# Longer pauses in the chain that makes the second FFN block's factors

## The chip, the core and the metric

The kernel runs on one core of a Trainium2 chip. Its engines each work through their own row of instructions, in the order in which the program gives them: TensorE (PE, matmuls, and PEld for its weight loads), VectorE (DVE), ScalarE (ACT), GpSimd (POOL) and SyncE (SP), which here issues all DMA transfers. The metric is device time in microseconds (us); less is better.

## The reference

One layer of a streaming encoder over 2048 prompt frames and 64 sample frames, 2112 tokens of width 1024: a gated delta-rule group and a pooling group with a common output projection, then a SwiGLU feed-forward part (FFN) of inner width 2816. The change touches the FFN and what prepares it.

```python
x = x + jnp.concatenate([o_delta, o_pool], axis=-1) @ w_out
h = rmsnorm(x, norm2_w)
x = x + (jax.nn.silu(h @ w_gate) * (h @ w_up)) @ w_down
```

All is computed in float32. Each operand of a matmul is split into a high part (a cast to float32r) and the rest, and three matmuls make one product.

## The kernel before

**Blocks and features.** The FFN runs over three blocks of 704 tokens, each in two halves of 352. The inner width is cut into 22 features of 128 columns. For a feature, gate and up are made together as a 2 x 2 by 2 x 2 product in Strassen's way (Winograd's form): seven products of 12 matmuls of 128x352 instead of eight, with three accumulators `px`, `py` and `pz` (`gate_up`, L1606). A product may be added to `px` again only after the sum so far has been copied out: ACT copies it to `g` or `u` (`COPY g<-px`), DVE adds the rest later, ACT makes the sigmoid in three steps (`ACTIVATE hr`), and DVE multiplies into `hr`.

**Weights.** A feature's weights come by DMA as raw tiles (`wr`, loads `wr<-in_wg_dram` and `wr<-in_wu_dram`). In the first block POOL makes the four sums S1 to S4 of them (`wrS`), ACT casts each to its high part, DVE subtracts for the low part (`ws`, `wsS`), and SP stores the split sums to DRAM (`gS<-wsS`) for the later blocks. Raw and split tiles live in small sets of buffers: a load or a cast waits until the old content has been read, and where the old content is also stored, until that store has landed (`prep_strassen`, L614).

**Down projection.** After every two features POOL makes four sums of the finished `hr` (`q<-hr`, and one in place), which ACT and DVE split into factors `hq` (`factors`, L1666). Groups of four features (one of two) are then multiplied by the down weights. For most groups this too is done in Strassen's way, with split sums that were made beforehand and are loaded straight from DRAM (`wsdS<-dsd`), beside raw tiles `wrd` that ACT and DVE split to `wsd` (`load_down`, L675). Group zero is features 0 to 3, group one 4 to 7, group two 8 to 11, group three 12 to 15. In the first block groups one to three are multiplied one feature pair late: group one follows feature 9, group two feature 13.

**The chain.** A block needs its tokens normalised and combined before its first feature: four row pairs of tiles, each with the seven factors 11, T1, T2, 21, T3, 22, T4. For the second block this runs as a chain of steps beside the first block's features (`stats2`, L1416, called by `between`, L1715, from feature 2 on). After the sums of squares, each of four turns (k = 0 to 3) loads four tiles (`xd<-x2d`), scales them on DVE (`xd<-xd,nw,r`), makes four differences on POOL (`xt<-xd,xd`, `xd<-xd,xd`, `xt<-xd,xt`) and stores seven tiles (`hpd<-xd`, `hpd<-xt`). The tiles come from a set of four buffers (`XBUFS["xs"]`). The second block reads them back through `load_h` (L1504) after the last feature of the first.

**What sets the order.** The program is not emitted as written. Every operation is noted by a recording layer (`Machine`), which places the operations of all engines with costs of its own, each engine taking the operation of lowest rank among those it holds ready; rank is mostly the place in the written order. Where the chain's steps are written is set by pauses: a chain gives back a number of us (`yield LAT_APPLY`, L1437 to L1457, five in each turn), and its next step is written once that much of matmul time has been written on PE. `LAT_APPLY` is 1.69.

Of the kernel before, what the change touches and what calls it, by code (L numbers as in the profile page):

```python
# [11 lines left out]
F32 = mybir.dt.float32  # L12
F32R = mybir.dt.float32r
# [5 lines left out]
P = 128  # L19
D = 1024  # L20
KT = D // P
# [19 lines left out]
TB2 = NTOK // NB2  # L41
# [3 lines left out]
PX = PB[0] + 2 * HP + DEC  # L45
# [322 lines left out]
def hybrid_kernel(ctx, tc, a, o):  # L368
# [128 lines left out]
    for G in FGROUPS:  # L497
        groups.append((f0, G))
        f0 += G
    plan, pres = [], [("pre", m, *groups[gi]) for gi in PRE[0] for m in range(KT // 2)]  # L500

    def with_pres(j, keys):

# [7 lines left out]
    for j in range(NBLK):  # L511
# [5 lines left out]
        else:  # L517
# [8 lines left out]

    dsd = {(f0, m): dpool.tile([4, P, 512], F32, tag=f"dsd{f0}_{m}", name=f"dsd{f0}_{m}")
           for f0, G in (groups[gi] for gi in PRE[0]) for m in range(KT // 2 * G // 4)}

    def halves(b, gi):  # L530

# [32 lines left out]
    def prep():  # L564
        key = plan[state["at"]]
        state["at"] += 1
        if key[0] == "pre":
            return pre_down(*key[1:])
        if key in stored and key[0] != "gu":
            parts = []  # L570
            for i in range(2):
                t = wtiles(f"p{i}")[1]()
                nc.sync.dma_start(out=flat(t), in_=wsd[key[0]][key[1], i])
                parts.append(t)
        elif key[0] == "wl":
            raw, parts = (f() for f in wtiles("l"))
            nc.sync.dma_start(out=raw, in_=wpd[key[1]] if key[2] else a["wout"][key[1]][:, :512])
            wsplit(parts, raw)
        elif key[0] in ("win", "wout"):
            parts = []  # L580
            for i in range(2):
                raw, t = (f() for f in wtiles(f"p{i}"))
                src = a[key[0]][key[1]][:, 512 * i : 512 * i + 512]
                nc.sync.dma_start(out=raw, in_=wpd[key[1]] if key[0] == "wout" and i else src)
                if key == ("win", 0):

                    r3, h3, l3 = (x.rearrange("p (k c) -> p k c", c=P) for x in (raw, t[:, 0], t[:, 1]))
                    nc.gpsimd.memset(l3[:, :, 64:].bitcast(F32), 0.0)
                    nc.scalar.copy(l3[:, :, :64], r3[:, :, :64])
                    nc.scalar.copy(h3[:, :, :64], r3[:, :, :64])  # L590
                    tt(h3[:, :, 64:], r3[:, :, 64:], l3[:, :, :64].bitcast(F32), ALU.subtract)
                else:
                    wsplit(t, raw)
                parts.append(t)
            if len(key) == 2:
                due.append((key, [(wsd[key[0]][key[1], i], t) for i, t in enumerate(parts)]))
        elif key[0] == "dn":
            _, m, f0, G = key
            raw, parts = (f() for f in wtiles("d", m % 2 == 0))
            nc.sync.dma_start(out=raw[:, : G * P], in_=a["wd"][m][:, f0 * P : (f0 + G) * P])  # L600
            wsplit(parts, raw, G * P, nc.vector)
        elif key[0] == "ds":
            parts = load_down(*key[1:4]) if key[4] else prep_down(*key[1:4])
        else:
            parts = prep_strassen(key)
        ready.append((key, parts))

        while due and due[0][0] != key:
            k, done = due.pop(0)
            for dst, t in done:  # L610
                nc.sync.dma_start(out=dst, in_=flat(t))
            stored.add(k)

    def prep_strassen(key):  # L614

        q = {f"{i}{j}": a[nm][key[1]][:, (j - 1) * 512 : j * 512]
             for i, nm in ((1, "wg"), (2, "wu")) for j in (1, 2)}
        raw, t, old = {}, {}, key in stored

        def get(nm, src):  # L620
            raw[nm] = wtiles(nm)[0]()
            nc.sync.dma_start(out=raw[nm], in_=q[src])

        if old:
            for i, nm in enumerate(FW):
                t[nm] = wtiles(nm, i % 2 == 1)[1]()
                if nm in gsd:
# [12 lines left out]
        gt(out=raw["S2"], in0=raw["S1"], in1=raw["11"], op=ALU.subtract)  # L640
        gt(out=raw["S4"], in0=raw["12"], in1=raw["S2"], op=ALU.subtract)
        for i, nm in enumerate(FW):
            t[nm] = wtiles(nm, i % 2 == 1)[1]()
            wsplit(t[nm], raw[nm], 512, nc.vector)
        due.append((key, [(gsd[nm][key[1]], t[nm]) for nm in FW if nm in gsd]))
        return t

    def pre_down(m, f0, G):

        n, was = G // 2 * P, machine.boost  # L650
        machine.boost = -PRE_LATE
        (tl, tr), (ll, lr) = ([t[:, i * n : i * n + n] for i in range(2)] for t in (
            names["poolw"], gp.tile([P, PX], F32, tag="pw", name=f"pr{f0}_{m}", bufs=2)[:, :512]))
        for t, m0 in ((tl, m), (ll, m + KT // 2)):
            both = bass.AP(t.tensor, t.offset, [list(t.ap[0]), [1, 2 * n]])
            nc.sync.dma_start(out=both, in_=a["wd"][m0][:, f0 * P : (f0 + G) * P])
# [7 lines left out]
        for i, x in enumerate((ll, lr, tl, tr)):  # L664
            parts = spare[i % len(spare)]
            split_w(parts.rearrange("p (q n) -> p q n", q=2), x)
            nc.sync.dma_start(out=dsd[f0, m][i], in_=parts.bitcast(F32))
        machine.boost = was

    def split_w(t, x):  # L670

# [744 lines left out]
    def stats2(b, pool, tag, tbufs):  # L1416

        r = cpool.tile([P, TB2], F32, tag="r", name=f"r{b}")
        src = stream_x(x2d, f"xd{b}_", TB2 * b)
        yield from rstd(f"n2_{b}", r, src, SUBS2, pool, tag, tbufs, nc.gpsimd)  # L1420
        yield 4.0
        gt = nc.gpsimd.tensor_tensor

        def put(nm, k, t):
            nc.sync.dma_start(out=hpd[b, FH.index(nm), k], in_=t)

        def get(k, i):
            t = src(k, N2 * i, N2)
            stt(t, t, n2w[:, k : k + 1], r[:, N2 * i : N2 * i + N2], ALU.mult, ALU.mult)
            return t  # L1430

        def new(nm, k):
            return wpool.tile([P, 512], F32, tag="xs", name=f"x{nm}{k}_{b}", bufs=XBUFS["xs"])[:, :N2]

        for k in range(4):
            b12, b22 = get(k, 1), get(k + 4, 1)
            yield LAT_APPLY  # L1437
            t3 = new("t3", k)
            gt(out=t3, in0=b22, in1=b12, op=ALU.subtract)
# [7 lines left out]
            yield LAT_APPLY  # L1447
# [5 lines left out]
            yield LAT_APPLY  # L1453
            t4 = new("t4", k)
            gt(out=t4, in0=b21, in1=t2, op=ALU.subtract)
            put("T4", k, t4)
            yield LAT_APPLY  # L1457

    heads = []
    blocks = []  # L1460
# [247 lines left out]


    fpos = {2: (0, 1), 4: (0, 2, 1, 3)}  # L1710
    six = [opool.tile([P, 3, 2, TB2], F32R, tag="op", name=f"h3_{i}", bufs=2) for i in range(2)]
    h3t = [six[i // 3][:, i % 3] for i in range(6)]
    h3, ys = {}, {}

    def between(b):  # L1715
# [78 lines left out]

STORE = 300e3

SLACK = 0.6
# [118 lines left out]
```

## Time and profile before

| | us |
|---|---|
| median of three runs | 2304.91 (2303.8 to 2306.77) |
| the profiled execution, as timed | 2305.54 |
| its span in the profile | 2303.8 |
| mean granted TensorE clock | 0.997 of full speed |

The profile is one execution. In its rows, buffer numbers are left out (`wsS<-wrS,wsS` is any split of a sum). A row in order of time gives start, length, engine, operation, tiles, how many in a row, and in brackets how long the engine had been idle before and what released it. A stretch gives each engine's busy time and, in brackets, its number of instructions. Between two stretches PE can be busy to the same share and have done fewer matmuls, because a matmul's record grows with a slow clock; the counts show it.

### The profile page before, as it was taken

The page shows a single profiled execution, that of the slowest core. Times are in us where ns is not written, and L with a number is a line of the kernel's source. Part 1 is how long each engine was busy: PE and PEld are TensorE (multiplying, and loading weights), DVE is VectorE, ACT ScalarE, POOL GpSimd, SP SyncE. Part 2 cuts the span into 40 slices and gives each one's busy share as a digit, 9 for nine tenths or more (in the row PEclk, how much of TensorE's full clock was granted, in tenths as well). Part 3 has the DMA queues.
Part 4 walks back from the last instruction along what each step waited for, and adds up shares of the span by engine and source line. Part 5 has one row for each costly group of instructions (what it writes and reads, how often), then busy time and mean ns, then how long its engine had stood idle before and what let it go on. Part 6 is the DMA issues. An engine that isn't in the chain of part 4 may idle for free.

```text
span 2303.8 us, 41539 instructions
## 1 busy us (share of the span) xinstructions
PE 2274.5 (99%) x14518; PEld 2134.6 (93%) x14518; DVE 1709.6 (74%) x3131; ACT 1342.5 (58%) x3036; POOL 829.9 (36%) x891
## 2 busy tenths in 40 slices
PE   8999999999999999999999999999999999999998
PEld 7998898888787888999999999999999999999998
DVE  7989866685678796788788777866667768666676
ACT  6987866684769864555346456554344574353344
POOL 3425342453246450555344236622111353010112
PEclk9999999999999999999999999999999999999999
DMA  8765586578476777867776578789765776666663
GB/s 287 262 187 188 203 292 233 194 238 275 158 248 230 213 211 256 304 239 247 256 258 223 187 254 294 254 262 313 241 192 199 261 279 225 210 216 224 210 196 104
DMA packets 256515, 536.96 MB, mean 233 GB/s; under 512 B 30001, under 2 KB 94001, under 8 KB 256305
## 3 DMA queue, kind: packets, MB, share of 16 engines
q1 hardware_dynamic: 256304, 534.30, 68.9%
q8 instruction: 114, 1.87, 0.3%
q14 instruction: 97, 0.79, 0.1%
HBM read 403.62 MB, written 130.58 MB: 232 GB/s over the span
## 4 chain that ended last, share of the span: by engine, by line
PE 91%; DVE 5%; ACT 1%; DMA 1%; issue 1%; POOL 1%; SPq 0%; POOLq 0%; DVEq 0%; ACTq 0%
PE px L283 21%; PE pp L283 18%; PE pz L283 13%; PE py L283 10%; PE dx L283 9%; PE dy L283 4%; PE d L283 3%; PE dz L283 2%; PE pk_p L283 2%; PE pt_p L283 2%; PE gr_p L283 1%; DVE y L283 1%; PE py_p L283 1%; DVE h L283 0%; PE px_p L283 0%
## 5 line engine op out<-in xcount | busy, mean ns | idle before, releaser
L283 PE MATMUL pp<-h,wsp 128*128 128x512 f32 (+1 forms) x2480 | 548.2, 364 | 10.5 <-DVE wsp L283 10.5
L283 PEld LDWEIGHTS pp<-h,wsp 128*128 128x128 f32 x2480 | 401.7, 190 | 58.9 <-ACT wsp L283 10.2
L283 ACT CAST ws<-wr 128x512 fp32r<-128x512 f32 x198 | 122.3, 618 | 172.1 <-PE dx L283 56.7
L283 DVE TENSOR_TENSOR ws<-wr,ws 128x512 fp32r<-128x512 f32 x198 | 170.3, 863 | 36.0 <-ACT ws L283 30.9
L283 POOL TENSOR_TENSOR q<-hr,hr 128x352 f32<-128x352 f32 x52 | 59.1, 1136 | 373.7 <-DVE hr L283 365.5
L283 ACT CAST wsd<-wrd 128x512 fp32r<-128x512 f32 (+1 forms) x120 | 62.5, 526 | 185.6 <-PE dx L283 65.9
L283 PE MATMUL pz<-op,wsp 128*128 128x288 f32 (+1 forms) x768 | 163.0, 353 | 0.0
L283 DVE TENSOR_TENSOR y<-y,dx 128x352 f32<-128x352 f32 x240 | 121.6, 516 | 55.8 <-PE dx L283 54.6
L283 PE MATMUL px<-hA,ws 128*128 128x352 f32 x792 | 144.9, 322 | 0.0
L283 PE MATMUL px<-hBT,wsS 128*128 128x352 f32 x792 | 139.6, 325 | 4.6 <-ACT g L283 4.6
L283 PE MATMUL py<-hA,wsS 128*128 128x352 f32 x792 | 141.9, 322 | 1.4 <-ACT wsS L283 1.0
L283 PE MATMUL py<-hB,wsS 128*128 128x352 f32 x792 | 142.3, 323 | 0.0
L283 ACT ACTIVATE hr<-g 128x352 f32<-128x352 f32 x132 | 65.6, 497 | 130.3 <-DVE g L283 129.9
L283 PE MATMUL pz<-hB,ws 128*128 128x352 f32 x792 | 140.9, 322 | 0.5 <-DVE ws L283 0.5
L283 ACT CAST TV_p<-pt_p 128x512 f16<-128x512 f32 x192 | 110.3, 588 | 50.0 <-PE pt_p L283 49.6
L283 PE MATMUL px<-hA,wsS 128*128 128x352 f32 x792 | 138.4, 322 | 0.1
L283 PE MATMUL px<-hBT,ws 128*128 128x352 f32 x792 | 137.7, 322 | 0.0
L283 PEld LDWEIGHTS px<-hBT,wsS 128*128 128x128 f32 x792 | 130.3, 190 | 5.2 <-ACT g L283 5.2
L283 PEld LDWEIGHTS pz<-op,wsp 128*128 128x128 f32 x768 | 120.9, 188 | 12.1
L283 PEld LDWEIGHTS py<-hA,wsS 128*128 128x128 f32 x792 | 129.3, 188 | 2.1 <-ACT wsS L283 1.3
L283 PEld LDWEIGHTS py<-hB,wsS 128*128 128x128 f32 x792 | 130.2, 189 | 0.0
L283 PEld LDWEIGHTS px<-hA,ws 128*128 128x128 f32 x792 | 130.0, 188 | 0.1
(693 smaller groups left out, 5769.5 us busy)
## 6 DMA issues: line engine op xcount, KB each, us to landing
wsS<-gS SPq DMA_DIRECT2D x176, 512.0 KB, 4.4
wsp<-wnd SPq DMA_DIRECT2D x126, 512.0 KB, 3.8
gS<-wsS SPq DMA_DIRECT2D x88, 512.0 KB, 5.2
wsdS<-dsd SPq DMA_DIRECT2D x88, 512.0 KB, 4.4
wr<-in_wg_dram SPq DMA_DIRECT2D x132, 256.0 KB, 3.6
wnd<-wsp SPq DMA_DIRECT2D x42, 512.0 KB, 5.2
wrd<-in_wd_dram SPq DMA_DIRECT2D x68, 256.0 KB, 2.7
xd<-x2d SPq DMA_DIRECT2D x96, 176.0 KB, 3.9
```

What stands on the lines that cost most here:

```text
L283: getattr(getattr(self.nc, op.eng), name)(*args, **kw)
```

## The change

Two parts. First, in `stats2` the five pauses of each turn become `CALM` = 9 instead of `LAT_APPLY` = 1.69 for the second block (`b == 1`); the third block's chain keeps 1.69. Second, `pre_down` becomes `pre_sums`, which could also make gate/up sums ahead of the FFN for the features in a table `PRE_GU`; that table is empty, so those branches never run. The boost around it, whose size was 0, is left out, and the tiles `h3t` are made only if group zero is not done in Strassen's way, which is the case here.

```diff
-PRE_LATE = 0
+PRE_GU = ()
+CALM = 9
...
+    for gi, (f0, G) in enumerate(groups):
+        pres += [("pre", "gu", f, i) for f in range(f0, f0 + G) if f in PRE_GU for i in range(2)]
+        pres += [("pre", "dn", f0, m) for m in range(KT // 2) if gi in PRE[0]]
...
-        raw, t, old = {}, {}, key in stored
+        raw, t, old = {}, {}, key in stored or key[1] in PRE_GU
...
-    def pre_down(m, f0, G):
-        n, was = G // 2 * P, machine.boost
-        machine.boost = -PRE_LATE
+    def pre_sums(what, f, i):
+        n = 256
...
-        machine.boost = was
...
         gt = nc.gpsimd.tensor_tensor
+        pause = CALM if b == 1 else LAT_APPLY
...
         for k in range(4):
             b12, b22 = get(k, 1), get(k + 4, 1)
-            yield LAT_APPLY
+            yield pause
             t3 = new("t3", k)
             gt(out=t3, in0=b22, in1=b12, op=ALU.subtract)
             put("T3", k, t3)
             b11 = get(k, 0)
             put("11", k, b11)
-            yield LAT_APPLY
+            yield pause
...
-    h3t = [six[i // 3][:, i % 3] for i in range(6)]
+    h3t = [six[i // 3][:, i % 3] for i in range(6 * (0 not in STR0))]
```

Every engine keeps its instructions; their order differs from feature 6 of the first block to feature 18. The numbers at the end of names tell single tiles apart and differ between the two programs; `_157` is a weight of feature 8, `_158` of feature 9, `_159` and `_160` of down group one, `hr_7` and `q_7` belong to feature 7, and `xd_2`, `xd_6`, `xt_1` are the chain's.

DVE at the end of feature 7, before:

```order
L283 TENSOR_TENSOR g_0_7_3267<-py_7_3263,g_0_7_3267 128x352
L283 TENSOR_TENSOR ws_157_3221<-wr_157_3214,ws_157_3221 128x512
L283 TENSOR_TENSOR wsS_157_3222<-wrS_157_3215,wsS_157_3222 128x512
L283 TENSOR_TENSOR wsS_157_3223<-wrS_157_3217,wsS_157_3223 128x512
L283 TENSOR_TENSOR ws_157_3224<-wr_157_3213,ws_157_3224 128x512
L283 TENSOR_TENSOR ws_158_3238<-wr_158_3231,ws_158_3238 128x512
L283 TENSOR_TENSOR hr_7_3261<-hr_7_3261,g_0_7_3267 128x352
L283 TENSOR_TENSOR hr_7_3261<-hr_7_3261,u_0_7_3266 128x352
```

And now:

```order
L283 TENSOR_TENSOR g_0_7_3248<-py_7_3242,g_0_7_3248 128x352
L283 TENSOR_TENSOR ws_157_3204<-wr_157_3197,ws_157_3204 128x512
L283 TENSOR_TENSOR wsS_157_3205<-wrS_157_3198,wsS_157_3205 128x512
L283 TENSOR_TENSOR wsS_157_3206<-wrS_157_3200,wsS_157_3206 128x512
L283 TENSOR_TENSOR hr_7_3240<-hr_7_3240,g_0_7_3248 128x352
L283 TENSOR_TENSOR hr_7_3240<-hr_7_3240,u_0_7_3247 128x352
```

The two products that finish feature 7's second half stand ahead of two weight splits that they stood behind.

POOL after feature 8's weights, before (`wrS_158` are feature 9's sums):

```order
L283 TENSOR_TENSOR xt_1_3189<-xd_6_1056_3173,xd_2_1056_3172 128x352
L283 TENSOR_TENSOR q_7_3270<-hr_7_3261,hr_6_3245 128x352
L283 TENSOR_TENSOR xd_2_1056_3172<-xd_2_1056_3172,xd_2_704_3190 128x352
L283 TENSOR_TENSOR wrS_158_3232<-wrS_158_3232,wr_158_3233 128x512
L283 TENSOR_TENSOR xt_1_3207<-xd_6_1056_3173,xd_2_1056_3172 128x352
L283 TENSOR_TENSOR wrS_158_3236<-wrS_158_3232,wr_158_3231 128x512
L283 TENSOR_TENSOR hr_6_3245<-hr_6_3245 128x352
L283 TENSOR_TENSOR wrS_158_3237<-wr_158_3234,wrS_158_3236 128x512
L283 TENSOR_TENSOR q_7_3271<-hr_7_3261,hr_6_3245 128x352
```

And now:

```order
L283 TENSOR_TENSOR q_7_3253<-hr_7_3240,hr_6_3226 128x352
L283 TENSOR_TENSOR hr_6_3226<-hr_6_3226 128x352
L283 TENSOR_TENSOR q_7_3254<-hr_7_3240,hr_6_3226 128x352
L283 TENSOR_TENSOR wrS_158_3213<-wrS_158_3213,wr_158_3214 128x512
L283 TENSOR_TENSOR q_7_3255<-hr_7_3240,q_7_3254 128x352
L283 TENSOR_TENSOR wrS_158_3217<-wrS_158_3213,wr_158_3212 128x512
L283 TENSOR_TENSOR wrS_158_3218<-wr_158_3215,wrS_158_3217 128x512
L283 TENSOR_TENSOR xt_1_3352<-xd_6_1056_3317,xd_2_1056_3316 128x352
```

The chain's three steps have left this place; the first of them now comes behind feature 9's last sum, the others later.

ACT around feature 9's copies of `px`, before:

```order
L283 ACTIVATE hr_9_3292<-hr_9_3292 128x352
L283 CAST wsd_159_3259<-wrd_159_3260 128x256
L283 ACTIVATE hr_8_3279<-g_0_8_3285 128x352
L283 CAST ws_158_3244<-wr_158_3233 128x512
L283 ACTIVATE hr_8_3279<-hr_8_3279,onec 128x352
L283 ACTIVATE hr_8_3279<-hr_8_3279 128x352
L283 CAST wsd_159_3255<-wrd_159_3256 128x512
L283 COPY g_0_9_3298<-px_9_3293 128x352
```

And now:

```order
L283 CAST ws_158_3225<-wr_158_3214 128x512
L283 COPY g_0_9_3279<-px_9_3276 128x352
L283 CAST wsd_159_3234<-wrd_159_3235 128x512
L283 COPY u_0_9_3280<-py_9_3277 128x352
L283 COPY g_0_9_3283<-px_9_3276 128x352
L283 CAST wsd_159_3238<-wrd_159_3239 128x256
L283 ACTIVATE hr_9_3275<-g_0_9_3279 128x352
```

The cast of 128x256, the first of the down group's last weight, stood six rows ahead of the second copy of feature 9's `px` and now stands behind it; feature 8's sigmoid and the split of feature 9's last weight are done before the first copy.

More of the change, by code (lines that the diff above doesn't have):

```diff
@@ L499, in hybrid_kernel @@
         f0 += G
-    plan, pres = [], [("pre", m, *groups[gi]) for gi in PRE[0] for m in range(KT // 2)]
+    plan, pres = [], []
+    for gi, (f0, G) in enumerate(groups):
+        pres += [("pre", "gu", f, i) for f in range(f0, f0 + G) if f in PRE_GU for i in range(2)]
+        pres += [("pre", "dn", f0, m) for m in range(KT // 2) if gi in PRE[0]]
     def with_pres(j, keys):
@@ L528, in hybrid_kernel @@
            for f0, G in (groups[gi] for gi in PRE[0]) for m in range(KT // 2 * G // 4)}
+    gpd = {(f, i): dpool.tile([4, P, 512], F32, tag=f"gpd{f}_{i}", name=f"gpd{f}_{i}") for f in PRE_GU for i in range(2)}
     def halves(b, gi):
@@ L567, in prep @@
         if key[0] == "pre":
-            return pre_down(*key[1:])
+            return pre_sums(*key[1:])
         if key in stored and key[0] != "gu":
@@ L626, in prep_strassen @@
                 t[nm] = wtiles(nm, i % 2 == 1)[1]()
-                if nm in gsd:
+                if nm in gsd and key[1] in PRE_GU:
+                    for j in range(2):
+                        nc.sync.dma_start(out=t[nm][:, :, 256 * j : 256 * j + 256].bitcast(F32),
+                                          in_=gpd[key[1], j][PRE_NM.index(nm)].rearrange("p (q n) -> p q n", q=2))
+                elif nm in gsd:
                     nc.sync.dma_start(out=flat(t[nm]), in_=gsd[nm][key[1]])
@@ L646, in prep_strassen @@
         return t
-    def pre_down(m, f0, G):
-        n, was = G // 2 * P, machine.boost
-        machine.boost = -PRE_LATE
+    def pre_sums(what, f, i):
+        n = 256
         (tl, tr), (ll, lr) = ([t[:, i * n : i * n + n] for i in range(2)] for t in (
[L653 to L656, printed above, removed]
+            names["poolw"], gp.tile([P, PX], F32, tag="pw", name=f"pr{what}{f}_{i}", bufs=2)[:, :512]))
+        if what == "dn":
+            for t, m0 in ((tl, i), (ll, i + KT // 2)):
+                both = bass.AP(t.tensor, t.offset, [list(t.ap[0]), [1, 2 * n]])
+                nc.sync.dma_start(out=both, in_=a["wd"][m0][:, f * P : f * P + 2 * n])
+            dst = dsd[f, i]
+        else:
+            for t, nm, at in ((tl, "wg", 0), (tr, "wg", 512), (ll, "wu", 0), (lr, "wu", 512)):
+                nc.sync.dma_start(out=t, in_=a[nm][f][:, at + i * n : at + i * n + n])
+            dst = gpd[f, i]
         gt = nc.gpsimd.tensor_tensor
@@ L1456, in stats2 @@
             put("T4", k, t4)
-            yield LAT_APPLY
+            yield pause
     heads = []
@@ L1710, in hybrid_kernel @@
     fpos = {2: (0, 1), 4: (0, 2, 1, 3)}
-    six = [opool.tile([P, 3, 2, TB2], F32R, tag="op", name=f"h3_{i}", bufs=2) for i in range(2)]
-    h3t = [six[i // 3][:, i % 3] for i in range(6)]
+    six = [opool.tile([P, 3, 2, TB2], F32R, tag="op", name=f"h3_{i}", bufs=2) for i in range(2 * (0 not in STR0))]
+    h3t = [six[i // 3][:, i % 3] for i in range(6 * (0 not in STR0))]
     h3, ys = {}, {}
@@ L1795 @@
 STORE = 300e3
+PRE_NM = ("S3", "S1", "S2", "S4")
 SLACK = 0.6
```

10 lines of the change are left out of this document (5 added, 5 removed).

## The prediction

> **What bounds the kernel now.** I read the page first (busy shares, the chain of waits), then the busy time by stretches around the place of the change, then the order of time there.
>
> ```profile
> PE 2274.5 (99%) x14518; PEld 2134.6 (93%) x14518; DVE 1709.6 (74%) x3131; ACT 1342.5 (58%) x3036; POOL 829.9 (36%) x891
> PE 91%; DVE 5%; ACT 1%; DMA 1%; issue 1%; POOL 1%; SPq 0%; POOLq 0%; DVEq 0%; ACTq 0%
> ```
>
> TensorE is busy for 99% of the span and makes 91% of the chain that ended last. So a change on other engines is worth what it adds to or takes from PE's gaps, and no more. The stretches of 10 us around the chain show where gaps are (columns: PE, PEld, DVE, ACT and POOL busy, each with its instructions, then PE's clock, DMA share, GB/s):
>
> ```profile
> 1070.00:1080.00 10.00, 10.00 (x64) 10.00 (x63) 7.68 (x14) 6.04 (x12) 2.98 (x3) 1.00 0.64 226
> 1080.00:1090.00 10.00, 8.49 (x51) 7.70 (x50) 9.86 (x9) 4.61 (x11) 9.92 (x9) 1.00 0.41 135
> 1090.00:1100.00 10.00, 8.10 (x51) 7.81 (x49) 5.90 (x11) 5.26 (x14) 2.20 (x2) 1.00 0.94 308
> 1100.00:1110.00 10.00, 7.29 (x31) 7.29 (x32) 5.49 (x11) 3.58 (x9) 0.93 (x1) 0.66 0.89 338
> ...
> 1140.00:1150.00 10.00, 10.00 (x65) 10.00 (x64) 10.00 (x15) 7.34 (x17) 4.57 (x3) 1.00 0.53 207
> ```
>
> A full stretch holds 64 or 65 matmuls. The three from 1080 to 1110 hold 51, 51 and 31: 133 of some 193, the only place in the first FFN block's gate/up work where PE loses more than a fraction of a microsecond. POOL stands at 9.92 of 10 in the first of them, DMA at 0.94 and 0.89 in the others. PE's own rows in order of time give the loss:
>
> ```profile
> 1078.12 2.08 PE L283 MATMUL pz<-hB,ws 128*128 128x352 f32 x12
> 1080.04 2.08 PE L283 MATMUL px<-hA,ws 128*128 128x352 f32 x12
> ...
> 1102.71 3.89 PE L283 MATMUL px<-hBT,wsS 128*128 128x352 f32 x12 [4.62 <-ACT g L283]
> 1106.40 2.36 PE L283 MATMUL py<-hB,wsS 128*128 128x352 f32 x10
> ...
> 1110.69 0.97 PE L283 MATMUL dx<-hq,wsd 128*128 128x352 f32 x5
> ```
>
> Twelve matmuls take 1.92 us from start to start (1078.12 to 1080.04), 0.16 each. From 1078.12 to 1110.69 PE runs twelve products of 12 and one matmul of the down group: 145, which is 23.2 us of work in 32.57. **Lost there: 9.4 us.** Of it 4.62 is one wait for ACT, about 2.4 the slow matmuls after it (3.89 for 2.08; 2.36 for ten that need 1.76) while the granted clock was 0.66 in the stretch, and the rest lies in 1080 to 1090.
>
> **Why PE waits there.** Feature 9's `px` adds its next product only after ACT has copied the sum out (`g<-px`):
>
> ```profile
> 1099.47 0.40 ACT L283 CAST wsd<-wrd 128x256 fp32r<-128x256 f32 x1 [4.68 <-DMA gS<-wsS]
> 1102.21 0.45 ACT L283 COPY g<-px 128x352 f32<-128x352 f32 x1
> ```
>
> The copy ends at 1102.66, PE starts at 1102.71. It was not late by itself: it stood in ACT's row behind the cast of a down weight (`wsd`), which needed a buffer whose old content, a split weight of feature 9, was still being stored (`gS<-wsS`). That store was issued late and landed late:
>
> ```profile
> 1085.67 3.38 SPq L283 DMA_DIRECT2D wrd<-in_wd_dram  x2
> 1091.15 0.42 SPq L283 DMA_DIRECT2D gS<-wsS  x1
> ...
> 1093.08 0.86 SPq L283 DMA_DIRECT2D gS<-wsS  x1
> ...
> DMA to landing us min/median/max: 5.8/8.2/8.3
> ```
>
> 1091.15 + 8.3 is 1099.45, where the cast starts. And SP was late because its two `wrd` loads wait for raw buffers that POOL's sums free:
>
> ```profile
> 1078.82 1.22 POOL L283 TENSOR_TENSOR q<-hr,hr 128x352 f32<-128x352 f32 x1 [5.41 <-DMA hpd<-xt]
> 1080.00 1.24 POOL L283 TENSOR_TENSOR xd<-xd,xd 128x352 f32<-128x352 f32 x1
> 1081.19 1.58 POOL L283 TENSOR_TENSOR wrS<-wrS,wr 128x512 f32<-128x512 f32 x1
> 1082.73 1.21 POOL L283 TENSOR_TENSOR xt<-xd,xd 128x352 f32<-128x352 f32 x1
> 1083.91 1.74 POOL L283 TENSOR_TENSOR wrS<-wrS,wr 128x512 f32<-128x512 f32 x1
> 1085.61 1.39 POOL L283 TENSOR_TENSOR hr<-hr 128x352 f32<-128x352 f32 x1
> 1086.96 1.74 POOL L283 TENSOR_TENSOR wrS<-wr,wrS 128x512 f32<-128x512 f32 x1
> 1088.65 1.24 POOL L283 TENSOR_TENSOR q<-hr,hr 128x352 f32<-128x352 f32 x1
> ```
>
> The middle sum ends at 1085.65 and the first load goes at 1085.67; the last ends at 1088.70, where the second goes (3.38 us for two issues). Two of the eight POOL rows, `xd` and `xt`, are steps of the chain that the change stretches: 2.45 us.
>
> **The change part by part.** *Names and the unused table.* `pre_sums` with an empty `PRE_GU` issues what `pre_down` issued, a boost of zero is left out, and the `h3` tiles are still made. No instruction moves: 0 us.
>
> *The pauses.* No instruction is added or removed. Of the chain's 16 scalings (DVE), 16 differences (POOL), 16 loads and 28 stores (SP), those of its third and fourth rows of tiles move later, into features 8 to 13 and down group one between them. What needs them is the second block, far away:
>
> ```profile
> L283 SPq DMA_DIRECT2D xh<-hpd x12: 319/379/688, 1368.9 to 1396.0; - x12
> L283 SPq DMA_DIRECT2D hpd<-xt x12: 320/430/502, 1019.2 to 1131.2; - x12
> ```
>
> The last store goes at 1131, the first load at 1369: 238 us of cover. The chain's last step now stands behind feature 13's sums instead of among feature 10's, three features of 84 matmuls at 0.16 or some 40 us later; that costs nothing at that end.
>
> *What goes away.* Three things follow from the new rows of the engines. First, feature 7's product is finished sooner, and with it POOL's first row above. These rows set it now:
>
> ```profile
> 1074.63 0.62 ACT L283 CAST ws<-wr 128x512 fp32r<-128x512 f32 x1 [0.41 <-PE px L283]
> 1075.16 0.49 ACT L283 ACTIVATE hr<-hr 128x352 f32<-128x352 f32 x1
> ...
> 1073.88 1.28 DVE L283 TENSOR_TENSOR wsS<-wrS,wsS 128x512 fp32r<-128x512 f32 x2
> 1075.29 0.69 DVE L283 TENSOR_TENSOR ws<-wr,ws 128x512 fp32r<-128x512 f32 x1
> 1077.06 0.69 DVE L283 TENSOR_TENSOR ws<-wr,ws 128x512 fp32r<-128x512 f32 x1 [1.07 <-DMA hpd<-xd]
> 1077.67 0.52 DVE L283 TENSOR_TENSOR hr<-hr,g 128x352 f32<-128x352 f32 x1
> 1078.22 0.53 DVE L283 TENSOR_TENSOR hr<-hr,u 128x352 f32<-128x352 f32 x1
> 1078.66 0.58 DVE L283 SCALAR_TENSOR_TENSOR xd<-xd,nw,r 128x352 f32<-128x352 f32 x1
> ```
>
> In the changed rows ACT's last step on `hr` stands ahead of that cast, and DVE's two `hr` products ahead of the two `ws` splits. DVE is free at 1075.16, so the products run from there for about 1.1 us and POOL's `q` starts near 1076.3 instead of 1078.82: 2.5 us sooner. Second, `xd` and `xt` are no longer between the sums. POOL then runs q, hr, q, wrS, q, wrS, wrS: 1.22 + 1.39 + 1.24 + 1.58 + 1.24 + 1.74 + 1.74 = 10.2 us (the third q taken as the others), so the last sum ends near 1086.5 instead of 1088.70, and the store goes near 1087.5 instead of 1091.15. Third and most, ACT's row now has both copies of feature 9's `px` ahead of the cast that waited. Even a store as late as before would no longer stand between PE and the copy. **Taken away: up to 9.4 us.**
>
> *What is late next.* PE no longer has feature 9's first products as filler ahead of feature 8's second, so it comes to that product at 1078.12 + 10 x 0.16 = 1079.7 and needs ACT's copy of feature 8's `px`, which stands behind a cast of POOL's `q`:
>
> ```profile
> 1080.09 0.48 ACT L283 CAST hq<-q 128x352 fp32r<-128x352 f32 x1
> ```
>
> With q at 1076.3 it is done at 1077.5; with the casts before it, its own 0.48 and the copy's 0.45, the copy ends near 1078.9: 0.8 us to spare. Were q as late as now (done at 1080.04), the copy would end near 1081.0 and PE lose 1.3. The next narrow place is feature 9. Its `px` is copied behind the cast of its last weight, which waits for the end of feature 8, 60 matmuls on (1089.3); with 0.62 for the cast and 0.45 for the copy that ends near 1090.5, and PE needs it 14 matmuls after 1089.3, at 1091.5. Then the down group, which PE reaches after 134 matmuls (1101.1): its second direct load takes a buffer that the next `gS` store frees. That store goes 1.9 us after the first now (1093.08), so near 1089.4; at 5.8 to 8.2 us it lands at 1095.2 to 1097.6, the load by a like time at 1101.0 to 1105.8, and PE comes to it 27 matmuls into the group, at 1105.4. That margin runs from 4.4 us to minus 0.4. I take 1.4 us as given back over these places (bounds 0 and 4.6, the longest wait in the rows), nearer to zero since each has a margin at nearly all durations shown.
>
> [...]
>
> *The sum.* The profiled execution has a span of 2303.8 and took 2305.54 with what lies around it. 2303.8 - 9.4 + 1.4 = 2295.8 of span, 2297.5 with the 1.7 around it; the median of the runs is 2304.91, 0.6 below that execution, so **2296.9 us**. Once for all: 0.2%, 4.6 us, is what a measurement of this kernel tells from no change.
>
> **The rivals.**
>
> *DVE becomes the bound in features 10 to 13.* DVE is at 10.00 in 1140 to 1150, with POOL at 4.57. Chain steps now fall there: about three of POOL (some 1.2 us each, during which a DVE split with two inputs can take longer) and two scalings of DVE of 0.58. If all of it adds to DVE, that is 4.8 us; PE would wait for split weights by that much less the slack of a product or so (1.9 us): 2.9 us, besides the 1.4. Time 2299.8, with a tail to 2303. Against it: DVE has 2 to 3 us free in each stretch of 10 on either side. [...]
>
> *The stall stays.* The DMA share of 0.94 and 0.89 and the 8.2 us landings could be the down group's own weights, which the change leaves alone. Then PE meets the same late store one step on, at the group's second load, and loses the 9.4 there: 2304.9. Against it: POOL's, SP's and ACT's rows each get earlier by themselves, and chain transfers leave that stretch.
>
> *Slower: the block by a store comes back at the second and third down groups.* PE's, ACT's and SP's rows are redrawn up to feature 18, so a cast that waits for a store can come to stand ahead of a copy that PE needs, at both groups. Each such block costs 9.4 by this one: 2304.9 - 9.4 + 2 x 9.4 = 2314.3. It decides where the store lands after PE's use, thus from 6 to 8 us after issue. For it: this is what a redrawn row did at group one. Against it: in the changed ACT row of group two the second copy of feature 13 stands ahead of the `wsd` cast from the same kind of buffer, and before the change PE has no gap in the stretches of both groups:
>
> ```profile
> 1200.00:1250.00 50.00, 50.00 (x314) 50.00 (x313) 43.05 (x70) 26.74 (x54) 18.21 (x14) 1.00 0.63 226
> 1250.00:1300.00 50.00, 50.00 (x314) 50.00 (x314) 39.38 (x67) 21.29 (x43) 13.42 (x10) 1.00 0.62 210
> ```
>
> **How the numbers follow.** The forecast, stall gone and small waits left: 0.66, own range 2294.5 to 2300. DVE as the bound: 0.16, about half of it still faster by over 0.2%. Stall stays: 0.09. Slower: 0.09. Faster: 0.66 + 0.07 = 0.73. Same: 0.09 + 0.08 = 0.17. Slower: 0.09 and a hundredth of the case before it, 0.10. The range runs from 2294.5 (nothing given back, and a microsecond of spread) to 2305.0, which takes in the DVE case and half of the stall that stays; about 0.06 lie below and 0.14 above.
>
> **What would show it.** The changed kernel's stretches from 1080 to 1110 should hold 64 matmuls each at a clock of 1.00, and PE's first down-group matmul should come near 1101. ACT's copies of feature 9's `px` should come ahead of the `wsd` cast, POOL's first `q` of feature 7 near 1076, the `gS` store near 1088. The chain's last store should come near 1170. The forecast is wrong if PE's rows show another wait of over 3 us between 1080 and 1300, or if the 4.62 stands again under another name.

## The result and the profile after

| | us |
|---|---|
| the kernel before, median of 7 runs | 2306.32 (2303.8 to 2307.97) |
| the changed kernel, median of 7 runs | 2299.15 (2297.74 to 2299.96) |
| ratio | 0.9967, 95% interval 0.9958 to 0.9977 |
| span of the profiled execution, before and now | 2303.8 and 2296.2 |

The change makes the kernel 0.33% faster, 7.2 us by these medians. The forecast was 2296.9 from a kernel before at 2304.91, thus 8.0 us less. Of the 2.2 us between forecast and result, 1.4 are the kernel before itself, whose median is 2306.32 over these seven runs and was 2304.91 over the first three.

The stretches of 10 us around the change, from the changed kernel (columns as in the prediction: busy time of PE, PEld, DVE, ACT and POOL, each with its instructions, then PE's clock, DMA share, GB/s):

```profile
1080.00:1090.00 10.00, 10.00 (x64) 10.00 (x63) 9.63 (x12) 6.57 (x15) 6.06 (x5) 1.00 0.51 147
1090.00:1100.00 10.00, 10.00 (x64) 10.00 (x63) 7.00 (x14) 5.20 (x11) 1.07 (x1) 1.00 0.99 348
1100.00:1110.00 10.00, 10.00 (x65) 10.00 (x64) 7.81 (x15) 2.40 (x5) 5.90 (x6) 1.00 0.79 247
...
1160.00:1170.00 10.00, 10.00 (x64) 9.95 (x63) 10.00 (x9) 6.60 (x16) 9.45 (x7) 1.00 0.45 143
```

In the first three, 64, 64 and 65 matmuls stand where there were 51, 51 and 31, all at a clock of 1.00. POOL's share in the first fell from 9.92 to 6.06. One stretch of 50 us holds the whole place in both kernels, however much their other parts shift it. First the kernel before, then the changed one:

```profile
1070.00:1120.00 50.00, 43.88 (x256) 42.79 (x255) 36.49 (x57) 22.18 (x46) 21.83 (x19) 0.93 0.67 231
```

```profile
1070.00:1120.00 50.00, 50.00 (x314) 50.00 (x313) 40.27 (x68) 24.14 (x50) 23.02 (x20) 1.00 0.79 264
```

58 matmuls more, at 0.16 us each: 9.3 us won here. This count is the yardstick for all experiments below: 314 means that nothing is lost in the 50 us, and each one missing is 0.16 us.

The two spans differ by 7.6 us, not by 9.3. Set side by side matmul by matmul, the changed kernel's execution is 0.6 us behind the other at 1070, 8.8 us ahead at 1120, 8.2 at 1300 and 7.6 at the end. The 0.6 is chance: up to feature 6 both programs have the same rows, and the first product of the FFN starts at 934.21 us in the one execution and at 935.15 in the other. The other 1.2 us are given back behind the place.

The rows of the changed kernel in order of time, one engine after the other (POOL, SP, ACT, PE):

```profile
1076.51 0.95 POOL L283 TENSOR_TENSOR q<-hr,hr 128x352 f32<-128x352 f32 x1 [5.11 <-DVE hr L283]
...
1079.97 1.73 POOL L283 TENSOR_TENSOR wrS<-wrS,wr 128x512 f32<-128x512 f32 x1
...
1082.85 1.57 POOL L283 TENSOR_TENSOR wrS<-wrS,wr 128x512 f32<-128x512 f32 x1
1084.50 1.64 POOL L283 TENSOR_TENSOR wrS<-wr,wrS 128x512 f32<-128x512 f32 x1
```

```profile
1084.45 0.88 SPq L283 DMA_DIRECT2D wrd<-in_wd_dram  x2
1085.42 0.38 SPq L283 DMA_DIRECT2D wsdS<-dsd  x1
1085.86 0.46 SPq L283 DMA_DIRECT2D gS<-wsS  x1
```

```profile
1094.28 0.45 ACT L283 COPY g<-px 128x352 f32<-128x352 f32 x1 [1.47 <-PE px L283]
1094.63 0.41 ACT L283 CAST wsd<-wrd 128x256 fp32r<-128x256 f32 x1
...
1099.15 0.62 ACT L283 CAST wsd<-wrd 128x512 fp32r<-128x512 f32 x1 [0.73 <-DMA gS<-wsS]
```

```profile
1099.84 2.08 PE L283 MATMUL px<-hBT,ws 128*128 128x352 f32 x12
1101.76 1.12 PE L283 MATMUL dx<-hq,wsd 128*128 128x352 f32 x6
```

The last sum ends at 1086.14 instead of 1088.70, and SP does not even wait for it: the second `wrd` load, which went at the end of that sum, now follows the first at once (0.88 us for two issues instead of 3.38). The store goes at 1085.86 instead of 1091.15, and ACT's copy comes without a wait for any store. The stores land faster too. Landing times of the four `gS` stores there, in the changed kernel:

```profile
DMA to landing us min/median/max: 4.8/5.2/6.5
```

Before the change the median was 8.2. The first of the four, which frees the cast's buffer, took 6.5 us instead of 8.2. What PE lost later, up to 1300, is one short wait:

```profile
1231.16 2.19 PE L283 MATMUL px<-hBT,wsS 128*128 128x352 f32 x12 [0.20 <-ACT g L283]
```

### The profile page after: what moved, and what is told of

It is laid out like the page before. It is cut to its first block, busy times and chain, and to the rows that moved or that the text cites. A ratio compares the mean times of both kernels' runs of the same rounds, so it can differ in the third digit from the quotient of the medians.

```text
span 2296.2 us, 41545 instructions
## 1 busy us (share of the span) xinstructions
PE 2271.3 (99%) x14518; PEld 2131.9 (93%) x14518; DVE 1714.4 (75%) x3131; ACT 1340.5 (58%) x3036; POOL 830.0 (36%) x891
## 4 chain that ended last, share of the span: by engine, by line
PE 89%; DVE 5%; DMA 2%; ACT 2%; issue 1%; POOL 1%; SPq 0%; POOLq 0%; DVEq 0%; ACTq 0%
PE px L283 21%; PE pp L283 17%; PE pz L283 13%; PE py L283 10%; PE dx L283 8%; PE dy L283 4%; PE d L283 3%; PE dz L283 2%; PE pk_p L283 2%; PE pt_p L283 2%; PE gr_p L283 1%; DVE y L283 1%; PE py_p L283 1%; DVE h L283 1%; DMA wnd<-wsp 0%
## 5 line engine op out<-in xcount | busy, mean ns | idle before, releaser
L283 PE MATMUL dy<-hq,wsdS 128*128 128x352 f32 x672 | 129.6, 322 | 0.7 <-DMA wsdS<-dsd 0.7
```

Source lines behind the costliest of these rows:

```text
L283: getattr(getattr(self.nc, op.eng), name)(*args, **kw)
```

## Experiments

That the pauses do all of it needs no run: with `CALM` set to 1.69 the changed program gives the rows of the kernel before on every engine, tile names aside, and the kernel before with the pauses alone gives those of the changed kernel. The first six experiments therefore move single rows. `find` picks an operation from the finished list by its engine and the names of its tiles, and `behind` puts it, with what depends on it, behind another; everything else keeps its place. `_157` is feature 8, `_158` feature 9, `_159` down group one.

| kernel | median us | ratio to before, 95% interval | matmuls in 1070 to 1120 | lost there, us |
|---|---|---|---|---|
| before | 2306.32 | | 256 | 9.3 |
| changed (`CALM` 9) | 2299.15 | 0.9967 (0.9958 to 0.9977) | 314 | 0 |
| one cast behind the copy | 2306.91 | 1.0004 (0.9995 to 1.0013) | 265 | 7.8 |
| both casts behind the copy | 2305.0 | 0.9997 (0.9988 to 1.0006) | 262 | 8.3 |
| POOL's two chain steps later | 2300.83 | 0.9981 (0.9973 to 0.999) | 290 | 3.8 |
| the same, product first | 2300.96 | 0.9976 (0.9966 to 0.9986) | 287 | 4.3 |
| the same, split sooner | 2300.79 | 0.9978 (0.9969 to 0.9987) | 295 | 3.0 |
| changed, cast first | 2297.97 | 0.9967 (0.9955 to 0.998) | 314 | 0 |
| `CALM` 4 | 2301.91 | 0.9982 (0.9973 to 0.999) | 284 | 4.8 |
| `CALM` 12 | 2298.88 | 0.9969 (0.9957 to 0.998) | 314 | 0 |
| `CALM` 15 | 2303.54 | 0.9987 (0.9978 to 0.9996) | 310 | 0.6 |

Each ratio is to runs of the kernel before that were taken beside it: their median is 2306.12 for "one cast", "POOL's two chain steps", "cast first" and `CALM` 15, 2305.49 for "both casts" and 2306.57 for the rest. The counts are of one profiled execution each, and one stretch of 3.4 us at half clock more or less makes 1.7 us in them (last section).

### ACT's row alone: one cast, then both

```diff
+    cast = find(out, "scalar", "wsd22_159")
+    copy = find(out, "scalar", "g2_0_9_", "px_0_9_")
+    behind(out, cast, copy)
```

> The kernel before with one step moved: ACT's cast of 128x256 (wsd, the last weight of down group one) and DVE's subtraction after it stand behind the second copy of feature 9's px, not six rows ahead of it. POOL, SP and PE keep their rows, the chain its place. My theory (the cast, blocked by a late store, stood ahead of a copy that PE needs): the gS store still goes near 1091 and lands near 1099.4, but PE no longer waits for it, so the wait of 4.62 us and the slow matmuls after it go (7.0 us together) and the 2.4 us lost in 1080 to 1090 stay: 7.0 us under the kernel before, near 2299.3 against 2306.3. Rival one (the store alone decides, wherever the cast stands): PE meets it some us later in the down group, gain under 2 us. Rival two (PE's own row, which is as before, makes the gap): no gain.

No gain: a miss. ACT's rows, then PE's, of this kernel:

```profile
1102.01 0.62 ACT L283 CAST wsd<-wrd 128x512 fp32r<-128x512 f32 x1 [4.18 <-DMA gS<-wsS]
1102.53 0.45 ACT L283 COPY g<-px 128x352 f32<-128x352 f32 x1
```

```profile
1103.03 2.69 PE L283 MATMUL px<-hBT,wsS 128*128 128x352 f32 x12 [3.82 <-ACT g L283]
```

A second `wsd` cast stood between the first and the copy, and it waits for the next `gS` store in the same way. So both were moved:

```diff
+    for name in ("wsd22_159", "wsd11_159"):
+        behind(out, find(out, "scalar", name), copy)
```

> The kernel before with both casts of down group one's first weights (wsd of 128x256 and of 128x512, with their DVE subtractions) behind the second copy of feature 9's px. With the first of them moved alone, the second stood in its place: it waited 4.18 us for the next gS store, and the copy with it. My theory, mended (it is any cast ahead of the copy that waits for one of feature 9's late stores): now nothing ahead of the copy waits, PE's wait there goes with the slow matmuls after it (7.0 us), the 2.4 us in 1080 to 1090 stay, and the down group's first weight, cast near 1102.5, is split by 1103.5, when PE comes to it near 1104: 2299 to 2301. Rival (the late store decides, wherever the casts stand): PE meets it in the down group some us later and waits 3 us or more there, 2303 to 2306.

Again no gain, and the rival was right, except that PE meets the late store before the down group and waits 2.80 us for it. ACT's copy is free now (it ran at 1097.30), but the block has gone one engine on. The row of ACT with both casts, DVE's rows, then PE's:

```profile
1101.74 0.93 ACT L283 CAST wsd<-wrd 128x512 fp32r<-128x512 f32 x2 [4.00 <-DMA gS<-wsS]
```

```profile
1102.70 0.42 DVE L283 TENSOR_TENSOR wsd<-wrd,wsd 128x256 fp32r<-128x256 f32 x1 [4.18 <-ACT wsd L283]
...
1105.07 0.51 DVE L283 TENSOR_TENSOR u<-px,u 128x352 f32<-128x352 f32 x1
```

```profile
1105.63 3.89 PE L283 MATMUL px<-hBT,ws 128*128 128x352 f32 x12 [2.80 <-DVE u L283]
```

DVE's subtraction of the 128x256 weight, one of the two whose casts were moved, waits for that cast, and the addition that empties `px` stands five rows behind it. Both times the next row in order waited for a late store. Some 2 us of the loss are not the stores': before the change and in both of these kernels, 51 matmuls stand in the stretch from 1080 to 1090.

### POOL's two chain steps alone

Their two stores on SP, which depend on them, move with them.

```diff
+    store = find(out, "sync", "gS1_", "wsS1_158")
+    last = out.index(find(out, "gpsimd", "wrS1_158", "wr22_158"))
+    steps = [op for op in out[last - 20 : out.index(store)] if op.eng == "gpsimd" and arg_names(op)[0].startswith("x")]
+    for op in steps[::-1]:
+        behind(out, op, store)
```

> The kernel before with two steps moved: the chain's xd and xt steps that stood between feature 9's sums on POOL (2.45 us), with their two stores on SP, stand behind the issue of the gS store. ACT, DVE and PE keep their rows, so the cast still stands ahead of the copy. My theory: the last sum ends near 1086.3 instead of 1088.70, the store goes near 1088.7 instead of 1091.15, the cast and the copy come 2.4 us sooner, and PE's wait falls from 4.62 to some 2 us if PE is no earlier itself; the time 2.4 us under the kernel before, up to 5 us if the slow matmuls go with the longer wait. Rival one (only the cast's place decides, the store lands late in any case because of the down group's own weights): the wait stays near 4.6, no gain. Rival two (the chain's POOL steps are all there is to it): the full 9 us.

34 of the 58 lost matmuls come back, 5.4 us. The wait at the copy is gone altogether, where 2 us of it had been expected to stay. The rows of SP and of ACT, and the stores' landing times, of this kernel:

```profile
1088.48 0.43 SPq L283 DMA_DIRECT2D gS<-wsS  x1
```

```profile
1095.16 0.39 ACT L283 CAST wsd<-wrd 128x256 fp32r<-128x256 f32 x1
```

```profile
DMA to landing us min/median/max: 4.4/4.9/5.2
```

The store goes at 1088.48 as worked out (1088.7), but lands in about 5 us, not 8.2, so the cast runs at 1095.16 with no wait. What is left is another wait, at another place. DVE's rows and PE's:

```profile
1081.64 1.60 DVE L283 TENSOR_TENSOR hq<-q,hq 128x352 fp32r<-128x352 f32 x1
1083.16 1.41 DVE L283 TENSOR_TENSOR ws<-wr,ws 128x512 fp32r<-128x512 f32 x1
```

```profile
1084.63 2.37 PE L283 MATMUL pz<-hB,ws 128*128 128x352 f32 x10 [2.00 <-DVE ws L283]
1086.79 2.86 PE L283 MATMUL py<-hA,wsS 128*128 128x352 f32 x10
```

PE waits 2.00 us for a weight of feature 9 that DVE splits late, in 1.41 us beside a busy POOL where such a split took 0.69 beside an idle one, and then runs 3.4 us at half clock, which is some 11 matmuls of these 20. Two further kernels tried to take that rest. The first makes feature 7's product sooner, as the changed kernel does:

```diff
+    last_hr = [op for op in out if op.eng == "scalar" and arg_names(op)[0].startswith("hr0_7_")][-1]
+    behind(out, find(out, "scalar", "ws22_157"), last_hr)
+    done = find(out, "vector", "hr0_7_", "u2_0_7_")
+    for name in ("ws11_158", "ws22_157"):
+        behind(out, find(out, "vector", name), done)
```

> The kernel with POOL's two chain steps moved, and besides the other thing that the prediction named: ACT's last step on feature 7's hr ahead of one cast, and DVE's two products on it ahead of two ws splits, as in the changed kernel. With the steps alone, 3.9 us stayed: PE waited 2.0 us for DVE's split of feature 9's third weight (ws, 1083.16 to 1084.57, behind three hq splits that took 0.8 to 1.6 each beside a busy POOL, 0.52 beside an idle one), then ran 3.3 us at half clock. My prediction counted the earlier product as a gain: POOL's q some 1.8 us sooner, all behind it too, and most of the 3.9 goes: 2297 to 2298.5. Rival (DVE's row has no room there: the two ws splits now run beside POOL, at 1.4 instead of 0.69 each): the split that PE waits for is no earlier or later, 2300 to 2303.

No gain over the steps alone: 287 matmuls for 290. PE's wait is for the same split:

```profile
1088.20 3.30 PE L283 MATMUL pz<-hB,ws 128*128 128x352 f32 x10 [2.52 <-DVE ws L283]
```

The second moves one DVE row behind two others:

```diff
+    split = find(out, "vector", "ws12_158")
+    row = [op for op in out if op.eng == "vector"]
+    behind(out, row[row.index(split) - 1], find(out, "vector", "wsS1_158"))
```

> The kernel with POOL's two chain steps moved, and one more row: DVE's third hq split (q) stands behind the split of feature 9's third weight (ws) and that of its first sum (wsS), for which PE waits there. My reading: the ws split ends 1.5 us sooner (near 1083.0) and PE waits 0.5 to 1 us instead of 2.0; if the clock stays at 1.00 then, 3 us less than with the steps alone, near 2298; if a wait of that size still halves it, 1.5 us less, near 2299.5. Rival (PE waits there for feature 8's sums, not for this split): no change, 2300.8.

The wait fell from 2.00 to 0.83 and the clock stayed at 1.00, as expected, but waits of 0.64 and 0.39 us for ACT's and DVE's next rows came up behind it, and 3.0 of the 3.8 us stayed. The time, 2300.79, is the one that the rival gave, though PE did wait for this split.

### The cast ahead again, with the store early

```diff
+    cast = find(out, "scalar", "wsd22_159")
+    copy = find(out, "scalar", "g2_0_9_", "px_0_9_")
+    behind(out, copy, cast)
```

This one starts from the changed kernel.

> The changed kernel with two neighbours in ACT's row exchanged: the cast of 128x256 stands ahead of the second copy of feature 9's px again. All else as in the changed kernel. My theory: the gS store that frees the cast's buffer goes at 1085.9 there, 5.3 us sooner than before the change, and lands by 1094.2 even at 8.3 us; PE needs the copy by 1096.0, so PE waits for under 0.5 us: the time of the changed kernel, 2299 (2298 to 2300). Rival one (the cast's place decides): the wait comes back at 3 us or more, 2303 to 2306.

314 matmuls, and the time of the changed kernel. ACT's rows:

```profile
1095.23 0.41 ACT L283 CAST wsd<-wrd 128x256 fp32r<-128x256 f32 x1
1096.81 0.45 ACT L283 COPY g<-px 128x352 f32<-128x352 f32 x1 [1.16 <-PE px L283]
```

The cast ahead of the copy runs without a wait, and the copy waits only for PE. With the two kernels on ACT's row this makes the square complete: with a late store either row of ACT loses 7.8 to 9.3 us, with an early one either row loses nothing. The store's time decides, the cast's place in ACT's row does not.

### Other pauses

```diff
-CALM = 9
+CALM = 4
```

and the same with 15, which ran first, and with 12.

> The changed kernel with CALM = 4. One chain step (xd) stands among feature 9's sums on POOL instead of two, a third stands ahead of them; ACT's row is that of the kernel before in this place, both casts ahead of the copy. My theory (the store's time decides): store about 1.2 us sooner than before the change, so the wait at the copy falls from 4.62 to 3 to 3.5 us: 2303 to 2305. If the time goes with the number of chain steps in the sums' way: half of the gain, 2302.5. Rival (any new order is as good): 2299.

> The changed kernel with CALM = 12. No chain step stands among feature 9's sums, and both casts stand ahead of the copy. With 15 the wait at the copy was gone, but 4.3 us came back at 1152, 1167 and 1172 in features 11 to 13, where ACT's copies of px waited behind splits that DVE finished late beside POOL. My theory: no wait over 1 us before 1110, and of the later waits some, since the chain's steps stand at 10 to 14 here too: 2299 to 2303. If the later waits belong to pauses above 9 as such: 2303. If they were a chance of the order with 15: 2299.

> The changed kernel with CALM = 15 instead of 9. No chain step stands among feature 9's sums on POOL, two of the sums stand ahead of the first q, but ACT's row is that of the kernel before in this place: the cast of 128x256 four rows ahead of the copy, and PE takes feature 9's first products early as before. My theory: sums, loads and store are so much sooner (store near 1086) that the cast is not blocked when PE needs the copy: 2299 within 1.5. Rival one (the cast's place decides): the wait of 4 to 5 us stays, 2304 to 2306. Third: the chain's later end (20 pauses of 15 us) costs something at the end of the block: above 2301 with a gap after 1300.

With 4 the wait at the copy was gone, not 3 us as my reading had it: the store went at 1086.32, 4.8 us sooner than before the change instead of 1.2. PE lost 4.8 us, for the most part in two other waits, 1.5 us for a split sum and 1.7 us in the down group, so the time is about that of the second reading (2302.5), though not by way of the copy. With 12 nothing is lost before 1120 and one wait of 0.6 us comes later: as good as 9. With 15 the place itself is nearly clean too (310), but features 11 to 13 pay, and the time is 4.5 us above the 2299 that was expected. The stretches of that kernel:

```profile
1150.00:1160.00 10.00, 9.18 (x58) 8.89 (x57) 8.78 (x15) 6.42 (x14) 2.90 (x3) 1.00 0.80 281
1160.00:1170.00 10.00, 9.02 (x54) 8.23 (x54) 9.90 (x11) 5.64 (x12) 7.97 (x6) 1.00 0.73 275
1170.00:1180.00 10.00, 9.02 (x56) 8.73 (x56) 9.98 (x14) 6.72 (x15) 5.68 (x5) 1.00 0.78 241
```

168 matmuls where 192 or 193 fit: 4 us. In the first of these, ACT's rows and PE's show how:

```profile
1151.90 0.49 ACT L283 CAST hq<-hr 128x352 fp32r<-128x352 f32 x1 [3.51 <-DVE hr L283]
...
1152.64 0.46 ACT L283 COPY g<-px 128x352 f32<-128x352 f32 x1
```

```profile
1153.15 2.18 PE L283 MATMUL px<-hBT,wsS 128*128 128x352 f32 x12 [0.82 <-ACT g L283]
```

PE waits for a copy that stands in ACT's row behind a cast of an `hr` that DVE finishes late; DVE is at 9.90 and 9.98 in the two stretches behind. That is a full DVE, as in the prediction's rival, and the time, 2303.5, is the tail given for it (2303). But the rival was reckoned for a pause of 9 and put down to chain steps, and of POOL's rows from 1145 to 1175 only three are chain steps, the others sums of weights and of `hr`. What fills DVE there was not taken apart, and that the times agree is luck.

### What a wait of PE costs

The changed kernel with the second copy of feature 9's `px` repeated n more times, which only delays what PE waits for (one execution of each):

```diff
+    copy = find(out, "scalar", "g2_0_9_", "px_0_9_")
+    at = out.index(copy)
+    for i in range(n):
+        again = Op()
+        again.eng, again.call = copy.eng, copy.call
+        out.insert(at, again)
```

> The changed kernel with ACT's second copy of feature 9's px done eight more times (the same copy, 0.34 us each), which only delays PE at the product behind it. The copy has 1.3 us to spare, so PE waits 0.34 x 8 - 1.3 = 1.4 us. If the clock halves only after a longer wait: 1.4 us lost. If a wait of this size is enough: 1.4 and about 1.7 for 3.4 us at half clock.

> As the kernel with eight more copies, with twelve: PE waits 2.8 us. One stretch at half clock after a wait of 2.0 us was seen in the kernel with POOL's two chain steps moved (3.3 us at 0.50): then 2.8 and 1.7 us are lost. [...]

> As before with eighteen more copies: PE waits 4.8 us, near the 4.62 of the kernel before the change. There 6.7 us stood at half clock, 4.9 of them in work: 2.4 us lost besides the wait. If that is what such a wait costs: 7.2 us lost in all. If the clock comes back after one stretch of 3.4 us whatever the wait: 4.8 and at most 1.7.

The repeated copies start 0.48 us apart, not 0.34, each after the end of the one before, so the waits came out longer: 2.50, 4.44 and 7.34 us. 297, 275 and 257 matmuls stand in the 50 us: 2.7, 6.2 and 9.1 us lost, so 0.2, 1.8 and 1.8 besides the wait. What the clock does after them is in the last section.

## Why the prediction was right, point by point

- **The place and its worth: right.** 9.4 us were said to be lost between 1078 and 1111, and 9.3 came back. The three stretches are full at a clock of 1.00, and PE reaches the down group at 1101.76 (said: near 1101).
- **Names and unused table at nothing: right**, as the rows show.
- **First, feature 7's product sooner.** The size was right: POOL's `q` at 1076.51 (said: 1076.3). Its worth was not: taken over by itself it won nothing beside POOL's two steps (287 matmuls for 290), since the DVE split that PE waits for there came no sooner.
- **Second, `xd` and `xt` out of the way of the sums: right, and undersized.** The last sum ended at 1086.14 (said: 1086.5). The store went 1.6 us sooner still than worked out (1085.86 for 1087.5), because the second load no longer waits for the last sum, which the prediction took for granted. These two rows of POOL, 2.45 us of work, with their two stores are worth 5.4 of the 9.3 us by themselves.
- **"Third and most, ACT's row now has both copies of feature 9's `px` ahead of the cast that waited. Even a store as late as before would no longer stand between PE and the copy."** This step failed. With ACT's row mended and the store as late as before, PE lost 8.3 us of the 9.3, now one engine on, at DVE's `u<-px`. The changed rows keep that order too: DVE's subtraction of the 128x256 weight stands two rows ahead of `u<-px`, and ACT's cast of 128x512 ahead of the second copy. (The changed kernel itself with a late store was not run.) The other way round the cast may stand ahead of the copy and costs nothing. The prediction read the row in which the wait showed as its cause. It had the chain behind it in full (POOL, SP, store), and the rival *the stall stays* even named what a late store would do ("one step on"); only the weight was laid on the wrong link. The sum held because the change makes the store early as well, and the 9.4 us were counted at the place, whatever their cause.
- **The landing time of 8.2 us** was carried over as fixed into what is late next and into the rivals. It fell to a median of 5.2 in the changed kernel, and to 4.9 with nothing moved but two POOL steps and their stores. So it belonged to that moment and not to a store as such; what made it 8.2 was not taken apart (the DMA share is 0.99 in the changed kernel's stretch too).
- **Given back, 1.4 us (bounds 0 and 4.6): the size came near, the places did not.** None of the three margins that were worked out ran out. Of the 1.2 us that the profiled execution gave back, 0.6 came by 1300, where the one wait in the rows is 0.20 us, and 0.6 later, where PE waits at 1830 for a down load:

```profile
1830.02 1.24 PE L283 MATMUL dy<-hq,wsdS 128*128 128x352 f32 x6 [0.65 <-DMA wsdS<-dsd]
```

The prediction had no row for that wait, so that 8.0 us less came this near to 7.2 is in part luck.
- **The slow matmuls at 2.4 us: right by the rows.** PE was back at 1102.71 and the clock at 1.00 at 1107.70: 5.0 us of work at half clock, 2.5 lost.
- **The chain's end.** Its last store goes at 1180.8, not near 1170. It costs nothing, as said: what reads it comes after the block's last feature. The group of the chain's last `xt` stores, from 1140 on, in the changed kernel (how many, shortest, median and longest issue in ns, first and last start):

```profile
L283 SPq DMA_DIRECT2D hpd<-xt x2: 522/836/1151, 1147.8 to 1180.8; - x2
```

- **DVE as the bound, 0.16:** not with a pause of 9, where the stretch from 1160 to 1170 has DVE at 10.00 and POOL at 9.45, and PE has its 64 matmuls all the same. With 15 it is what decides. The gain does not grow with the pause: 4, 9, 12 and 15 give 2301.9, 2299.2, 2298.9 and 2303.5.
- **Slower, a store's block at groups two and three, 0.09:** nothing of it shows.

What stays open is the rest of 3.0 to 3.8 us that POOL's two steps do not take. The changed kernel and `CALM` 12 lose none of it; in both, PE takes the weight of feature 9 whose split it waited for later than before, so DVE has time for it. That PE's row alone would take the rest was not tried.

## What to carry to other kernels

When an engine waits in its row for a buffer, ask what made the buffer late before moving the row: here each mended row handed a late store on to the next row, while two small operations taken off another engine's path to that store gave more than half of the gain. The operations to look for are those without a deadline that a scheduler has put between steps with one. Spreading them out helps until they meet the next stage that has no room, so the pause is to be tried at a few sizes, and each one looked at where it puts the work and not only at where it took it from.

## What was not expected of the hardware

**After a wait the clock stood at half for 0, 3.4 or 6.8 us, and the length of the wait does not say which.** In the stretches of 1 us it reads 1.00 or 0.50, and lies between only where it changes, so one with a mean clock c is counted as 2(1 - c) us at half clock. In such stretches, the kernel with both casts moved, after PE's wait of 2.80 us:

```profile
1104.00:1105.00 1.00, 0.00 (x0) 0.00 (x0) 1.00 (x3) 0.26 (x1) 0.00 (x0) 0.84 0.91 314
1105.00:1106.00 1.00, 0.37 (x1) 0.37 (x2) 1.00 (x4) 0.14 (x1) 0.69 (x1) 0.50 0.97 351
...
1110.00:1111.00 1.00, 1.00 (x5) 1.00 (x4) 0.68 (x2) 0.00 (x0) 0.00 (x0) 0.50 1.09 287
1111.00:1112.00 1.00, 1.00 (x6) 1.00 (x6) 0.96 (x2) 0.00 (x0) 0.00 (x0) 0.74 0.72 128
```

That is 0.32 + 6 + 0.52 = 6.8 us. With eight more copies there is none at all after 2.50 us:

```profile
1098.20 2.18 PE L283 MATMUL px<-hBT,wsS 128*128 128x352 f32 x12 [2.50 <-ACT g L283]
```

```profile
1098.00:1099.00 1.00, 0.80 (x5) 0.80 (x6) 0.51 (x2) 0.46 (x2) 0.00 (x0) 1.00 0.94 357
```

All waits of 2 us and over that the runs had here:

| PE's wait, us | kernel | time at half clock, us |
|---|---|---|
| 2.00 | two chain steps later | 3.4 |
| 2.50 | eight more copies | 0 |
| 2.52 | the same steps, product first | 3.4 |
| 2.80 | both casts moved | 6.8 |
| 3.82 | one cast moved | 3.4 |
| 4.44 | twelve more copies | 3.4 |
| 4.62 | before | 6.8 |
| 7.34 | eighteen more copies | 6.8 |

What decides it was not shown. The half clock began 1.9 to 5.3 us after PE had stopped: before the change at 1100.87, 2.8 us into the wait of 4.62, and it ended at 1107.70, 5.0 us after PE was back. In three of the seven kernels that had one it began only when PE was at work again: with two chain steps later 1.2 us after the wait, with one cast moved 1.5, with twelve more copies 0.5. After the shorter waits the clock stayed at 1.00: after 1.7 and 1.5 us with `CALM` 4, after 1.01 and 0.49 us with one cast moved, after 0.83 us with the split sooner.

Since part of the slow time can fall into the wait itself, the cost beside the wait was between 0.2 us (after 2.50) and 2.9 us (after 2.80, where PE was back at 1105.63 and 5.9 us at half clock were left).

**DVE beside POOL.** In the kernel with two chain steps later a split of 128x352 took 0.51 us with an idle POOL (at 1091.69) and one of 128x512 0.69 us (at 1076.80); beside a busy POOL they took up to 1.60 and 1.41 us in the rows above. Before the change it is 0.69 (at 1077.06) and 1.42 us (at 1083.07) for one of 128x512. So a split on which PE waits was longer beside POOL's steps, here by 0.7 us.
